# Deeper weight prefetch, 128-row bias matmuls and fewer GpSimd steps in a two-block transformer kernel

## The chip, the cores and the metric

The kernel runs on one core of a Trainium2 chip. The metric is the time of one execution on the device in microseconds. A core has five engines, each of which runs its own list of instructions in order: PE (matrix products), DVE (vectors), ACT (activations and scaled copies), POOL (GpSimd) and SP, which here only issues transfers. They wait for each other through semaphores. The DMA engines move data between HBM and the core's memory. A tile pool gives out a fixed number of buffers; a transfer into a buffer waits until its last reader is done.

## The reference

Two blocks follow each other on 512 tokens of width 1024. The first one mixes tokens with a two-directional RWKV-7 recurrence (8 heads of 64, over 256 context and 512 latent tokens) and a Fourier mix, then runs a mixture of 32 experts, top 4. The second one has two layers with three attention branches.

The recurrence, per step:

```python
sa = jnp.einsum('bhij,bhj->bhi', s, aa_t)        # aa = -kk
s = s * w_t[..., None, :] + sa[..., :, None] * bb_t[..., None, :] + v_t[..., :, None] * k_t[..., None, :]
y_t = jnp.einsum('bhij,bhj->bhi', s, r_t)
```

with `w = exp(-exp(-softplus(-w_log) - 0.5))`, whose logarithm is a constant times a sigmoid, and `a = sigmoid(...)`. An expert computes, for its tokens:

```python
u = xb @ w1[e] + b1[e]                           # 1024 -> 2048
glu = jnp.minimum(u[:, 0::2], 7.0)
lin = jnp.clip(u[:, 1::2], -7.0, 7.0)
act = glu * jax.nn.sigmoid(1.702 * glu) * (lin + 1.0)
y = act @ w2[e] + b2[e]                          # 1024 -> 1024
```

All weights are float32.

## The kernel before

The program runs through stages that show in the profile: projections (to about 160 us), the recurrence (160 to 660), output projection and routing (to 960), the experts (to 2330), the second block (to the end).

**Recurrence.** The 768 positions are six units of 128 per direction; units 0 and 1 are the context. A unit is prepared by closures in `unit()`: `lora(i)` makes the sigmoids `sw` and `a` as 0.5·tanh+0.5 (tanh on ACT, the affine on POOL, line 624), `expo1` the running sum `cum` of `sw` inside chunks of 64 (DVE scan) and on POOL the exclusive sum `cum − sw` (line 632), `expo2` three exponentials on ACT (e1 and e2 of ±cum, e3 of the exclusive sum, line 639), `keys1` to `keys4` the decayed keys: `kd`, `bk` (lines 654, 655, DVE) and `ar`, whose two halves of 64 partitions are multiplied on DVE (first) and POOL (second): lines 662 (keys by e3) and 668 (r by e1). Then follow small Gram products on PE, an inversion by substitution on DVE (lines 723, 725) with transfers in between, and the chain over chunks that carries the state (PE with POOL `pst`, line 824, and DVE). A table of positions orders the closures of different units against each other.

**Experts.** Experts are ranked by token count at run time. Rank decides the room: 192 tokens (6 experts), 128 (9, called whole) or 64 (17). Their weights come as parts of 2 × 128 rows by 512 columns, 512 KB each, 24 per expert (16 for w1, 8 for w2), 768 in all. `sequence()` and `order(g)` write out which chunks of which two to four experts alternate. Class `Weights` gives the parts in that order: `ahead()` issues loads on SP into a pool of seven raw tiles, then splits up to three parts ahead into a high half (ACT copy to fp32r, `whi`, line 1326) and a low half (DVE difference, `wlo`, line 1330), in a pool of four pairs. Parts of whole experts are used raw by PE (line 1705). `ahead()` is called at each `next()`, so in the program a load stands at most seven parts before its use; the scheduler then places each engine's instructions by priority.

For a chunk of w1, `up()` opens the PSUM tile with the bias, as a matmul: the stationary side is the expert's column of a permutation matrix, repeated (`permr`, or `mhalf` with zeros in its second half of columns for 64-token blocks, whose high and low products lie in two halves of PSUM), the moving side is `mb`, all experts' biases with 32 rows of high halves and 32 of low ones, so 64 rows (line 1837). The products follow (lines 1709, 1710, 1712). `swiglu()` then runs gl (DVE, 1727), ln (DVE, 1728), sg (ACT, 1729), ln (DVE, 1730), ln (POOL, 1731), and two PE transposes of ln (line 1690), whose copy is the input of w2. The second block has its own `Weights` with three raw tiles.

Of the kernel before, what the change touches and what calls it, by code (L numbers as in the profile page):

```python
# [8 lines left out]
F = mybir.dt.float32  # L9
# [89 lines left out]
class Blk1:  # L99
# [494 lines left out]
    def unit(self, u):  # L594
# [11 lines left out]
        def lora(i):  # L606
            def f():
                w, src, nm = ((self.w2[0], self.lw, "sw"), (self.w2[1], self.la, "a"))[i]
                dst = S[nm] = self.tt(nm)
                for d in range(2):  # L610
# [9 lines left out]
                    for hp in range(4):  # L620

                        nc.scalar.activation(dst[:, hp, 2 * d:2 * d + 2, :].rearrange("p n t -> p (n t)"), p[:, hp * 128:(hp + 1) * 128], AF.Tanh,
                                             bias=self.hb[:, i * 8 + d * 4 + hp:i * 8 + d * 4 + hp + 1], scale=0.5)
                nc.gpsimd.tensor_scalar(dst, dst, 0.5, 0.5, op0=OP.mult, op1=OP.add)
            return f

        def expo1():
            sw = S["sw"]
            c = S["c"] = self.tt("cum")
            for hp in range(4):  # L630
                nc.vector.tensor_tensor_scan(c[:, hp].rearrange("p n t -> p (n t)"), self.rst, sw[:, hp].rearrange("p n t -> p (n t)"), 0.0, OP.mult, OP.add)
            nc.gpsimd.tensor_tensor(sw, c, sw, op=OP.subtract)

        def expo2():
            sw, c = S["sw"], S["c"]
# [21 lines left out]
        def keys3():  # L657
            ar = S["ar"] = self.ubuf(u, [128, 4, 2, 4, 2, 64], "ar")
            kn = S["kn"]
            for h, e in ((0, nc.vector), (1, nc.gpsimd)):  # L660
                p = slice(h * 64, h * 64 + 64)
                e.tensor_tensor(ar[p, :, h, :, 0, :], kn[p], S["e3"][p], op=OP.mult)

        def keys4():
            ar, r = S["ar"], S["r"]
            for h, e in ((0, nc.vector), (1, nc.gpsimd)):
                p = slice(h * 64, h * 64 + 64)
                e.tensor_tensor(ar[p, :, h, :, 1, :], r[p], S["e1"][p], op=OP.mult)
            nc.gpsimd.tensor_tensor(S["kd"], S["kd"], r, op=OP.mult)
            nc.sync.dma_start(self.prD[:, u - 2].rearrange("p h d t -> p (h d t)"), S["kd"].rearrange("p h n t -> p (h n t)"))  # L670
# [625 lines left out]
class Weights:  # L1296
# [41 lines left out]

    reach = 4

    def ahead(self, loads, splits):
        while len(self.loads) < min(self.used + loads, len(self.parts)):
            m, k0 = self.parts[len(self.loads)][:2]
            self.loads.append(self.load(m(), k0))
        isplit = lambda j: self.parts[j][-1] is not False
        n = sum(isplit(j) for j in range(self.used, len(self.splits)))
        while len(self.splits) < min(len(self.loads), self.used + self.reach):
            j = len(self.splits)
            if isplit(j):
                if n >= splits:  # L1350
                    break
                n += 1
            self.splits.append(self.split(self.loads[j]) if isplit(j) else self.loads[j][0])

    def next(self, splits=None):
        self.ahead(self.nraw, self.nsplit if splits is None else splits)
        out = self.splits[self.used]
        self.used += 1
        return out


def consts_moe():
# [10 lines left out]
    lim = np.array([[float(max(128 * j, CAP[r])) if 128 * (j + 1) > CAP[r] else 1e6 for r in range(32) for j in range(4)]], np.float32)  # L1373
    two = np.concatenate([iota[:, :64], iota[:, :64]], 1)
    return {"m_cap": caps, "m_tri": tri, "m_tie": tie, "m_first": first, "m_iota": iota, "m_two": two, "m_tok": tok, "m_lim": lim}


class Moe:
# [13 lines left out]
    def consts(self):  # L1392
# [8 lines left out]
        nc.sync.dma_start(self.iota, rowbc(I["m_iota"], 512))  # L1401
        self.two = c.tile([128, 128], F, name="mtwo")
        nc.sync.dma_start(self.two, rowbc(I["m_two"], 128))
        self.tokf = c.tile([128, 5], F, name="mtokf")
# [9 lines left out]
        nc.sync.dma_start(self.br, rowbc(I["b_router"][0:1, :], 32))  # L1414
        self.cap = c.tile([128, 32], F, name="mcap")
        nc.sync.dma_start(self.cap, rowbc(I["m_cap"], 32))
        self.wr = c.tile([128, 8, 32], F, name="mwr")
        nc.sync.dma_start(self.wr, I["w_router"][0].rearrange("(k p) e -> p k e", p=128))

    def consts2(self, pool):  # L1420

        nc, I, c = self.nc, self.i, self.c
        self.halves = [c.tile([64, 128], R, name=f"mhalf{a}") for a in range(2)]
        self.b1 = c.tile([64, 2048], R, name="mb1")
        zero = pool.tile([64, 128], F, name="mz", tag="mz", bufs=1)
        nc.gpsimd.memset(zero, 0.0)
        for t in self.halves:
            nc.gpsimd.tensor_copy(t, zero)
        for a in range(2):
            t = pool.tile([128, 1024], F, name="mb1r", tag="fxh", bufs=2)  # L1430
            s = slice(a * 1024, (a + 1) * 1024)
            t = t[0:32]
            nc.sync.dma_start(t, I["b1"][0][:, s])
            nc.scalar.activation(self.b1[0:32, s], t, AF.Copy)
            nc.gpsimd.tensor_tensor(self.b1[32:64, s], t, self.b1[0:32, s].bitcast(F), op=OP.subtract)

# [55 lines left out]
    def route(self):  # L1492
# [37 lines left out]
        nc.vector.tensor_scalar(perm, self.iota[:32, :E], rank, None, op0=OP.is_equal)  # L1530
        self.perm = c.tile([64, E], R, name="permr")
        nc.vector.tensor_copy(self.perm[0:32], perm)
        nc.vector.tensor_copy(self.perm[32:64], perm)
        dr = tt.tile([32, E], F, name="drank")
# [100 lines left out]
    def hots(self, r0, n, start, two, posm=None):  # L1635

        nc = self.nc
        iob = (self.two if two else self.iota)[:, None, :128].to_broadcast([128, n, 128])
        hot = []
        for t in range(4):  # L1640
            h = self.g.tile([128, 4, 128], BF, name="hot", tag="hot", bufs=4)
            src = (self.posm if posm is None else posm)[:, t, r0:r0 + n]
            if start:
                s2 = self.g.tile([128, 8], F, name="hots", tag="hots", bufs=4)
                nc.vector.tensor_scalar(s2[:, :n], src, -float(start), None, op0=OP.add)
                src = s2[:, :n]
            nc.vector.tensor_tensor(h[:, :n], iob, src[:, :, None].to_broadcast([128, n, 128]), op=OP.is_equal)
            hot.append(h)
# [65 lines left out]
    def swiglu(self, ps, act, c, tag=None):  # L1714
# [44 lines left out]
    def plan(self, before):  # L1759
# [23 lines left out]

        first = [(lambda m=m: [m], k0) for m, k0 in before]
        self.W.stream(first + sum([parts(r, a, cc) for g in sequence() for a, r, cc in order(g)], []))

    def experts(self, hD, x1, gt2):
# [38 lines left out]
        def up(r, cc):  # L1826
# [129 lines left out]
        self.overflow(hD)  # L1956
        gs = groups()
        where = {r: min(sum(not whole(q) for q in g[:j]), 1) for g in seq for j, r in enumerate(g)}
# [52 lines left out]
    def overflow(self, hD):  # L2011
# [9 lines left out]
        with tc.If(ne > 0):  # L2021
# [19 lines left out]
            with tc.For_i(0, 128, 1) as i:  # L2041
                te = x_.tile([1, 2], I32, name="te", tag="te", bufs=1)
                nc.sync.dma_start(te, tD[bass.ds(i, 1), :])
                on = nc.values_load(te[0:1, 0:1], min_val=0, max_val=1)
                with tc.If(on > 0):
                    e = nc.values_load(te[0:1, 1:2], engines=[ET.SP], min_val=0, max_val=31)
                    ix = x_.tile([128, 1], I32, name="ix", tag="ix", bufs=1)
                    nc.sync.dma_start(ix, iD[bass.ds(i, 1), :].rearrange("a p -> p a"))
# [25 lines left out]
            nc.vector.tensor_tensor(row, self.later[3], offs[:, None, :].to_broadcast([128, 4, 32]), op=OP.add)  # L2074

            over = c.tile([128, 4, 32], F, name="over")
            nc.vector.tensor_tensor(over, self.later[3], self.cap[:, None, :].to_broadcast([128, 4, 32]), op=OP.is_ge)
            gto = self.pick(over, "gto", x_, "y")
# [1034 lines left out]
```

## Time and profile before

| | |
|---|---|
| median of 3 runs | 3734.91 us (3721.79 to 3737.12) |
| profiled execution | 3737.26 us |
| its span, first to last instruction | 3735.5 us |
| mean granted TensorE clock | 0.930 |
| PE busy | 3393.0 us (91%) |
| DVE busy | 2464.9 us (66%) |
| ACT busy | 1698.0 us (45%) |
| POOL busy | 1034.5 us (28%) |
| splits on DVE, line 1330 | 736 instructions, 883.9 us |
| splits on ACT, line 1326 | 736 instructions, 769.9 us |
| POOL's SwiGLU step, line 1731 | 152 instructions, 179.9 us |
| loads of expert weights | 768 of 512 KB |

The busy share is an average over stages with different limits, so the views below are by stage. A granted clock of 1 is 2.4 GHz, half of it 1.2 GHz. In a timeline the distance between two starts on PE says what a matmul costs; its shown length overlaps the next one. "Idle before" names what the engine waited for; where two things were waited for it is the later one.

### The profile page before, as it was taken

How to read it: one execution, taken by the hardware profiler on the slowest of the kernel's cores; microseconds unless marked ns; L12 is line 12 of the kernel's file. 1: busy time of each engine (PE TensorE's matmuls, PEld its weight loads, DVE VectorE, ACT ScalarE, POOL GpSimd, SP SyncE). 2: the span in 40 equal slices, each digit the busy share in tenths (PEclk: the TensorE clock that was granted, in tenths of full speed). 3: DMA queues.
4: the chain of work that ended last, by engine and by line, in shares of the span. 5: the costliest groups of instructions: out<-in, count | busy, mean ns of one | idle time of the engine just before them, and what ended most of it. 6: DMA issues, size and time to landing. Idle time of an engine off the chain costs nothing. (4 is left out here: it accounts for less than half of the span.)

```text
span 3735.5 us, 50031 instructions
## 1 busy us (share of the span) xinstructions
PE 3393.0 (91%) x16864; PEld 2514.0 (67%) x16864; DVE 2464.9 (66%) x4793; ACT 1698.0 (45%) x2937; POOL 1034.5 (28%) x957
## 2 busy tenths in 40 slices
PE   7966689859799999999899999799999999999999
PEld 4746576645575566656566655588878878887887
DVE  6778865676786687766687766854566455456653
ACT  4634323224555565555566554444444334344442
POOL 4444232432111112020121202432332332324223
PEclk9986667969899999999999999899999999999999
DMA  7853234626878898878989787432221243222113
GB/s 254 269 148 83 61 75 123 210 103 222 268 230 292 285 310 298 256 268 273 306 268 334 245 301 268 142 87 74 85 71 51 68 152 86 77 77 80 40 52 107
DMA packets 420639, 653.79 MB, mean 175 GB/s; under 512 B 83939, under 2 KB 145568, under 8 KB 419862
## 3 DMA queue, kind: packets, MB, share of 16 engines
q1 hardware_dynamic: 414650, 633.32, 52.6%
q0 software_dynamic: 4000, 13.90, 1.2%
q10 hardware_dynamic: 1724, 3.28, 0.3%
q8 instruction: 136, 2.23, 0.2%
q14 instruction: 129, 1.06, 0.1%
HBM read 610.80 MB, written 39.61 MB: 174 GB/s over the span
## 5 line engine op out<-in xcount | busy, mean ns | idle before, releaser
L1330 DVE TENSOR_TENSOR wlo<-wraw,whi 128x1024 fp32r<-128x1024 f32 (+1 forms) x736 | 883.9, 1210 | 417.6 <-ACT whi L1326 404.3
L1326 ACT ACTIVATE whi<-wraw 128x1024 fp32r<-128x1024 f32 x736 | 769.9, 1057 | 616.2 <-DMA wraw<-in_w 153.2
L2279 PE MATMUL psg<-whi,xh 128*128 128x512 f32 (+1 forms) x1152 | 473.1, 411 | 0.0
L2281 PE MATMUL psg<-whi,xl 128*128 128x512 f32 (+1 forms) x1152 | 451.8, 392 | 0.0
L2280 PE MATMUL psg<-wlo,xh 128*128 128x512 f32 (+1 forms) x1152 | 450.3, 391 | 0.0
L1731 POOL TENSOR_TENSOR ln<-ln,sg 64x256 f32<-64x256 f32 (+1 forms) x152 | 179.9, 1184 | 884.1 <-DVE ln L1730 464.3
L1332 POOL TENSOR_TENSOR wlo<-wraw,whi 128x288 fp32r<-128x288 f32 x184 | 241.4, 1313 | 591.8 <-ACT whi L1326 549.9
L1709 PE MATMUL ps<-whi,x 128*128 128x512 f32 x928 | 389.2, 420 | 0.7 <-ACT whi L1326 0.7
L1710 PE MATMUL ps<-wlo,x 128*128 128x512 f32 x928 | 373.9, 403 | 8.3 <-DVE wlo L1330 8.0
L1705 PE MATMUL ps<-wraw,x 128*128 128x512 f32 x576 | 270.7, 621 | 0.0
L2281 PEld LDWEIGHTS psg<-whi,xl 128*128 128x128 f32 x1152 | 217.9, 189 | 42.3
L2279 PEld LDWEIGHTS psg<-whi,xh 128*128 128x128 f32 x1152 | 218.6, 190 | 34.9 <-ACT xh L2296 0.9
L2280 PEld LDWEIGHTS psg<-wlo,xh 128*128 128x128 f32 x1152 | 218.7, 190 | 34.6
L1709 PEld LDWEIGHTS ps<-whi,x 128*128 128x128 f32 x928 | 177.7, 191 | 72.1 <-issue 22.7
L1710 PEld LDWEIGHTS ps<-wlo,x 128*128 128x128 f32 x928 | 177.9, 192 | 50.1 <-DVE wlo L1330 15.2
L1710 PE MATMUL ps<-wlo,a 128*128 128x512 f32 x464 | 193.2, 417 | 6.6 <-DVE wlo L1330 6.6
L1705 PEld LDWEIGHTS ps<-wraw,x 128*128 128x128 f32 x576 | 109.3, 197 | 131.1 <-issue 130.2
L1709 PE MATMUL ps<-whi,a 128*128 128x512 f32 x464 | 193.9, 420 | 1.0 <-ACT whi L1326 1.0
L2419 ACT ACTIVATE pexp<-pss,mx 128x128 f32<-128x128 f32 x192 | 101.1, 527 | 154.7 <-DVE mx L2414 66.7
L1705 PE MATMUL ps<-wraw,a 128*128 128x512 f32 x288 | 136.5, 611 | 0.0
L1677 POOL DMA_INDIRECT xg<-hD,idxi x38 | 40.4, 1062 | 288.7 <-PE ps L1690 271.2
L1710 PEld LDWEIGHTS ps<-wlo,a 128*128 128x128 f32 x464 | 90.6, 195 | 36.9 <-DVE wlo L1330 14.9
(736 smaller groups left out, 6850.2 us busy)
## 6 DMA issues: line engine op xcount, KB each, us to landing
wraw<-in_w SPq DMA_DIRECT2D x768, 512.0 KB
wraw<-in_w_in SPq DMA_DIRECT2D x140, 512.0 KB
mraw<-in_w_ada SPq DMA_DIRECT2D x32, 512.0 KB
wraw<-in_w_out SPq DMA_DIRECT2D x24, 512.0 KB
wada<-in_w_ada SPq DMA_DIRECT2D x16, 512.0 KB
wraw<-in_w_mem_kv SPq DMA_DIRECT2D x16, 512.0 KB
wraw<-in_w_branch_m SPq DMA_DIRECT2D x8, 512.0 KB
wraw<-in_w_branch_b SPq DMA_DIRECT2D x8, 512.0 KB
```

The lines of the kernel that those rows point to most:

```text
L1326: nc.scalar.activation(hi, raw, AF.Copy)
L1330: nc.vector.tensor_tensor(lw[:, :m], rw[:, :m], hw[:, :m].bitcast(F), op=OP.subtract)
L1332: nc.gpsimd.tensor_tensor(lw[:, m:], rw[:, m:], hw[:, m:].bitcast(F), op=OP.subtract)
L1677: self.last = nc.gpsimd.indirect_dma_start(out=x[:n], out_offset=None, in_=hD, in_offset=bass.IndirectOffsetOnAxis(ap=idx, axis=0))
L1705: nc.tensor.matmul(ps, a, w[:, k], start=s, stop=e)
L1709: nc.tensor.matmul(ps, a, hi[:, k], start=s, stop=False)
L1710: nc.tensor.matmul(ps, a, lo[:, k], start=False, stop=e and not two)
L1731: nc.gpsimd.tensor_tensor(ln[:m], ln[:m], sg[:m], op=OP.mult)
L2279: nc.tensor.matmul(p, xh[:, kk], hi[:, k, :n], start=kk == 0, stop=False)
L2280: nc.tensor.matmul(p, xh[:, kk], lo[:, k, :n], start=False, stop=False)
L2281: nc.tensor.matmul(p, xl[:, kk], hi[:, k, :n], start=False, stop=kk == kch - 1)
L2419: nc.scalar.activation(p[:, :n], s[:, :n], AF.Exp, bias=nm, scale=-1.0, accum_out=H["d"][:, i:i + 1])
```

## The change

Four edits. Weight loads: eight raw tiles instead of seven, and `ahead()` issues loads, before and after the splits, until the tile that the next one reuses has not yet been split (or, for raw parts, used). Until the expert loop begins a limit holds the loads to seven parts past the first ones. First biases: `mb` holds columns 0 to 1023 in rows 0 to 63 and columns 1024 to 2047 in rows 64 to 127, and the permutation column is zero in the other 64 rows, so the matmul contracts over 128 rows; `mhalf` becomes two tiles per set, hence two POOL copies per expert that uses it. Memory for this comes from a broadcast iota and from sharing one tag for gl and sg. Recurrence: the affine goes to ACT, the exclusive sum and its exponential are dropped (the exclusive decay is e1 shifted by one position, with the first column copied), and both halves of keys3 and keys4 run on DVE.

```diff
@@ unit(), lora / expo1 / expo2 / keys3 / keys4
-                nc.gpsimd.tensor_scalar(dst, dst, 0.5, 0.5, op0=OP.mult, op1=OP.add)
+                nc.scalar.activation(dst, dst, AF.Copy, bias=0.5, scale=0.5)
...
-            nc.gpsimd.tensor_tensor(sw, c, sw, op=OP.subtract)
...
-            nc.scalar.activation(sw, sw, AF.Exp, scale=-KAP)
-            S["e3"] = sw
...
-            for h, e in ((0, nc.vector), (1, nc.gpsimd)):
+            for h in range(2):
                 p = slice(h * 64, h * 64 + 64)
-                e.tensor_tensor(ar[p, :, h, :, 0, :], kn[p], S["e3"][p], op=OP.mult)
+                nc.vector.tensor_tensor(ar[p, :, h, :, 0, 1:], kn[p, :, :, 1:], S["e1"][p, :, :, :63], op=OP.mult)
+                nc.gpsimd.tensor_copy(ar[p, :, h, :, 0, 0], kn[p, :, :, 0])
...
-            for h, e in ((0, nc.vector), (1, nc.gpsimd)):
+            for h in range(2):
                 p = slice(h * 64, h * 64 + 64)
-                e.tensor_tensor(ar[p, :, h, :, 1, :], r[p], S["e1"][p], op=OP.mult)
+                nc.vector.tensor_tensor(ar[p, :, h, :, 1, :], r[p], S["e1"][p], op=OP.mult)
@@ class Weights
-    def __init__(self, tc, ctx, raw=7, parts=4, kn=2, side="left"):
+    def __init__(self, tc, ctx, raw=8, parts=4, kn=2, side="left"):
...
     def ahead(self, loads, splits):
-        while len(self.loads) < min(self.used + loads, len(self.parts)):
-            m, k0 = self.parts[len(self.loads)][:2]
-            self.loads.append(self.load(m(), k0))
         isplit = lambda j: self.parts[j][-1] is not False
+        def fetch():
+            top = min(len(self.parts), self.limit or len(self.parts))
+            while len(self.loads) < top:
+                j = len(self.loads)
+                q = j - self.nraw
+                if j >= self.used + loads if loads else q >= 0 and q >= (len(self.splits) if isplit(q) else self.used):
+                    break
+                m, k0 = self.parts[j][:2]
+                self.loads.append(self.load(m(), k0))
+        fetch()
...
+        fetch()
     def next(self, splits=None):
-        self.ahead(self.nraw, self.nsplit if splits is None else splits)
+        self.ahead(0 if self.free else self.nraw, self.nsplit if splits is None else splits)
@@ Moe.consts2, Moe.swiglu, Moe.plan, up()
-        self.b1 = c.tile([64, 2048], R, name="mb1")
+        self.b1 = c.tile([128, 1024], R, name="mb1")
...
-        gl = x_.tile([128, 256], F, name="gl", tag="gl", bufs=2)
+        gl = x_.tile([128, 256], F, name="gl", tag="gl", bufs=3)
...
-        sg = x_.tile([128, 256], F, name="sg", tag="sgm", bufs=2)
+        sg = x_.tile([128, 256], F, name="sg", tag="gl", bufs=3)
...
+        self.W.free, self.W.limit = False, len(first) + 7
...
-                nc.gpsimd.tensor_copy(half[:, 0:64], self.perm[:, r:r + 1].bitcast(F).to_broadcast([64, 64]))
+                for a in range(2):
+                    nc.gpsimd.tensor_copy(half[a][:, 0:64], self.perm[:, a, r:r + 1].bitcast(F).to_broadcast([128, 64]))
...
-                        pm = half if xx.n == 64 else self.perm[:, r:r + 1].to_broadcast([64, 128])
-                        nc.tensor.matmul(p, pm, self.b1[:, cc * 512:(cc + 1) * 512], start=True, stop=False)
+                        pm = half[cc // 2] if xx.n == 64 else self.perm[:, cc // 2, r:r + 1].to_broadcast([128, 128])
+                        nc.tensor.matmul(p, pm, self.b1[:, cc % 2 * 512:(cc % 2 + 1) * 512], start=True, stop=False)
```

The change also moves instructions. On ACT, in the experts, this is the place whose `sg` for a 64-token block starts at 1317.18 us in the trace of before (whi: high half of a part; sg: sigmoid of SwiGLU; us: first half of a 64-token sum; a: transposed activations). Before:

```order
L1693 ACTIVATE a<-ps 128x2x64
L1326 ACTIVATE whi<-wraw 128x1024 x4
L1729 ACTIVATE sg<-gl 128x256
L1326 ACTIVATE whi<-wraw 128x1024 x3
L1720 ACTIVATE us<-ps 64x512
L1326 ACTIVATE whi<-wraw 128x1024 x2
L1693 ACTIVATE a<-ps 128x256
L1729 ACTIVATE sg<-gl 64x256
L1326 ACTIVATE whi<-wraw 128x1024
L1720 ACTIVATE us<-ps 64x512
```

After, where line 1738 is sg, 1729 is us and 1325 is whi:

```order
L1702 ACTIVATE a<-ps 128x2x64
L1325 ACTIVATE whi<-wraw 128x1024 x2
L1738 ACTIVATE sg<-gl 128x256
L1325 ACTIVATE whi<-wraw 128x1024 x4
L1729 ACTIVATE us<-ps 64x512
L1325 ACTIVATE whi<-wraw 128x1024 x3
L1702 ACTIVATE a<-ps 128x256
L1729 ACTIVATE us<-ps 64x512
L1325 ACTIVATE whi<-wraw 128x1024
L1738 ACTIVATE sg<-gl 64x256
```

Counted from the start of the experts, three more high halves now stand ahead of this sg, and so does the next block's us.

On POOL, in the recurrence, the preparation of the second latent unit between two steps of the chain (pst). Before:

```order
L624 TENSOR_SCALAR sw<-sw 128x1024
L624 TENSOR_SCALAR a<-a 128x1024
L632 TENSOR_TENSOR sw<-cum,sw 128x1024
L642 COPY pcc<-e_2760 128x16
L824 TENSOR_TENSOR pst<-sv,pcc 64x256 x2
L668 TENSOR_TENSOR ar<-r,e_2760 64x4x4x64
L662 TENSOR_TENSOR ar<-kn,sw 64x4x4x64
L824 TENSOR_TENSOR pst<-sv,pcc 64x256 x2
L649 TENSOR_TENSOR a<-a,kn 128x1024
L650 TENSOR_TENSOR kd<-kd,k 128x1024
```

After:

```order
L661 COPY ar<-kn 64x4x4 x2
L639 COPY pcc<-e_2757 128x16
L823 TENSOR_TENSOR pst<-sv,pcc 64x256 x4
L646 TENSOR_TENSOR a<-a,kn 128x1024
L647 TENSOR_TENSOR kd<-kd,k 128x1024
```

Five long operations leave POOL; the two products of keys3 and keys4 stand on DVE instead.

## Rows read from the trace of the kernel before

**Rows 1.** Table by stage: PE, PEld, DVE, ACT, POOL busy us (instructions), clock, DMA share, GB/s.

```profile
160.00:660.00 500.00, 375.91 (x3241) 306.10 (x3240) 363.74 (x774) 174.83 (x388) 193.84 (x179) 0.71 0.41 108
...
960.00:2330.00 1370.00, 1295.97 (x4767) 832.36 (x4768) 998.49 (x1444) 759.08 (x1046) 218.00 (x190) 0.97 0.83 280
```

**Rows 2.** Same view, a 50-us window of the experts.

```profile
1950.00:2000.00 50.00, 50.00 (x175) 30.52 (x174) 33.44 (x51) 27.44 (x39) 9.40 (x9) 1.00 0.97 338
```

**Rows 3.** Waits, 960 to 2330 us: engine, line, waited for: us, times, longest.

```profile
ACT whi L1326 <- DMA wraw<-in_w: 148.1, 133, 7.2
...
PE ps L1690 <- POOL ln L1731: 41.3, 15, 5.2
...
PE ps L1710 <- DVE wlo L1330: 14.5, 20, 3.1
```

**Rows 4.** Timeline, PE at 1676 us: start, length, instruction, count, [idle before <-releaser].

```profile
1676.43 0.44 PE L1690 MATMUL ps<-ident,ln 128*128 128x128 f32 x2 [3.75 <-POOL ln L1731]
...
1678.20 0.63 PE L1709 MATMUL ps<-whi,x 128*128 128x512 f32 x1
1678.63 0.63 PE L1710 MATMUL ps<-wlo,x 128*128 128x512 f32 x1
```

**Rows 5.** Same view, PE at 2101 to 2107 us.

```profile
2101.20 0.34 PE L1690 MATMUL ps<-ident,ln 64*128 64x64 f32 x2
2101.47 0.50 PE L1709 MATMUL ps<-whi,x 128*128 128x512 f32 x1
...
2104.46 0.33 PE L1690 MATMUL ps<-ident,ln 64*128 64x64 f32 x2
2104.61 0.48 PE L1837 MATMUL ps<-mb,permr 64*128 64x512 f32 x1
2105.01 0.50 PE L1709 MATMUL ps<-whi,x 128*128 128x512 f32 x1
...
2106.05 0.39 PE L1710 MATMUL ps<-wlo,x 128*128 128x512 f32 x1
2106.28 0.39 PE L1712 MATMUL ps<-whi,x 128*128 128x512 f32 x1
2106.60 0.50 PE L1837 MATMUL ps<-mb,mhalf 64*128 64x512 f32 x1
2107.03 0.50 PE L1709 MATMUL ps<-whi,x 128*128 128x512 f32 x1
```

**Rows 6.** Instructions of line 1837: count, shortest/median/longest ns, first and last start.

```profile
L1837 PEld LDWEIGHTS ps<-mb,mhalf x92: 182/183/336, 826.1 to 2284.2; 64*128 64x128 f32 x92
...
L1837 PE MATMUL ps<-mb,permr x60: 469/478/793, 822.5 to 2296.4; 64*128 64x512 f32 x60
```

**Rows 7.** Timeline, ACT at 1317 us.

```profile
1317.18 0.40 ACT L1729 ACTIVATE sg<-gl 64x256 f32<-64x256 f32 x1
...
1320.97 1.05 ACT L1326 ACTIVATE whi<-wraw 128x1024 fp32r<-128x1024 f32 x1
```

**Rows 8.** Groups by line, POOL, 160 to 660 us: count, busy us, mean ns, idle before.

```profile
L662 POOL TENSOR_TENSOR ar<-kn,sw 64x1024 f32<-64x1024 f32 x6 | 16.1, 2689 | 13.6 <-PE ps L867 12.1 <-issue 1.4
...
L632 POOL TENSOR_TENSOR sw<-cum,sw 128x1024 f32<-128x1024 f32 x6 | 14.7, 2456 | 18.3 <-DVE cum L631 11.5 <-DVE Fm L725 6.8
...
L668 POOL TENSOR_TENSOR ar<-r,e 64x1024 f32<-64x1024 f32 x4 | 10.7, 2666 | 0.2
...
L624 POOL TENSOR_SCALAR a<-a 128x1024 f32<-128x1024 f32 x6 | 6.6, 1101 | 3.3 <-ACT a L622 3.3
```

**Rows 9.** Same view, DVE, 160 to 660 us.

```profile
L654 DVE TENSOR_TENSOR bk<-a,e 128x1024 f32<-128x1024 f32 x6 | 13.7, 2279 | 10.3 <-POOL a L649 10.2
...
L668 DVE TENSOR_TENSOR ar<-r,e 64x1024 f32<-64x1024 f32 x4 | 13.0, 3249 | 0.0
...
L662 DVE TENSOR_TENSOR ar<-kn,sw 64x1024 f32<-64x1024 f32 x6 | 9.9, 1655 | 0.1
...
L655 DVE TENSOR_TENSOR bk<-kd,e 128x1024 f32<-128x1024 f32 x6 | 7.3, 1212 | 0.0
```

More of the change, by code (lines that the diff above doesn't have):

```diff
@@ L1337, in stream @@
         self.parts, self.loads, self.splits, self.used = parts, [], [], 0
-    reach = 4
+    reach, free = 4, True
+    limit = None
     def ahead(self, loads, splits):
-        while len(self.loads) < min(self.used + loads, len(self.parts)):
-            m, k0 = self.parts[len(self.loads)][:2]
-            self.loads.append(self.load(m(), k0))
         isplit = lambda j: self.parts[j][-1] is not False
+        def fetch():
[8 more added lines that the diff above has]
+        fetch()
         n = sum(isplit(j) for j in range(self.used, len(self.splits)))
@@ L1373, in consts_moe @@
     lim = np.array([[float(max(128 * j, CAP[r])) if 128 * (j + 1) > CAP[r] else 1e6 for r in range(32) for j in range(4)]], np.float32)
-    two = np.concatenate([iota[:, :64], iota[:, :64]], 1)
-    return {"m_cap": caps, "m_tri": tri, "m_tie": tie, "m_first": first, "m_iota": iota, "m_two": two, "m_tok": tok, "m_lim": lim}
+    return {"m_cap": caps, "m_tri": tri, "m_tie": tie, "m_first": first, "m_iota": iota, "m_tok": tok, "m_lim": lim}
 class Moe:
@@ L1401, in consts @@
         nc.sync.dma_start(self.iota, rowbc(I["m_iota"], 512))
-        self.two = c.tile([128, 128], F, name="mtwo")
-        nc.sync.dma_start(self.two, rowbc(I["m_two"], 128))
         self.tokf = c.tile([128, 5], F, name="mtokf")
@@ L1414, in consts @@
         nc.sync.dma_start(self.br, rowbc(I["b_router"][0:1, :], 32))
-        self.cap = c.tile([128, 32], F, name="mcap")
-        nc.sync.dma_start(self.cap, rowbc(I["m_cap"], 32))
         self.wr = c.tile([128, 8, 32], F, name="mwr")
@@ L1422, in consts2 @@
         nc, I, c = self.nc, self.i, self.c
-        self.halves = [c.tile([64, 128], R, name=f"mhalf{a}") for a in range(2)]
-        self.b1 = c.tile([64, 2048], R, name="mb1")
-        zero = pool.tile([64, 128], F, name="mz", tag="mz", bufs=1)
+        self.halves = [[c.tile([128, 128], R, name=f"mhalf{a}{b}") for b in range(2)] for a in range(2)]
+        self.b1 = c.tile([128, 1024], R, name="mb1")
+        zero = pool.tile([128, 1024], F, name="mb1r", tag="fxh", bufs=2)[:, :128]
         nc.gpsimd.memset(zero, 0.0)
-        for t in self.halves:
+        self.perm = c.tile([128, 2, 32], R, name="permr")
+        nc.gpsimd.tensor_copy(self.perm.rearrange("p c e -> p (c e)"), zero[:, :64])
+        for t in self.halves[0] + self.halves[1]:
             nc.gpsimd.tensor_copy(t, zero)
@@ L1431, in consts2 @@
             s = slice(a * 1024, (a + 1) * 1024)
[L1432 to L1435, printed above, removed]
+            p = slice(a * 64, a * 64 + 32)
+            nc.sync.dma_start(t[p], I["b1"][0][:, s])
+            nc.scalar.activation(self.b1[p], t[p], AF.Copy)
+            nc.gpsimd.tensor_tensor(self.b1[a * 64 + 32:a * 64 + 64], t[p], self.b1[p].bitcast(F), op=OP.subtract)
     def logits(self, t, hT):
@@ L1530, in route @@
         nc.vector.tensor_scalar(perm, self.iota[:32, :E], rank, None, op0=OP.is_equal)
-        self.perm = c.tile([64, E], R, name="permr")
-        nc.vector.tensor_copy(self.perm[0:32], perm)
-        nc.vector.tensor_copy(self.perm[32:64], perm)
+        for a in range(4):
+            nc.vector.tensor_copy(self.perm[a * 32:a * 32 + 32, a // 2], perm)
         dr = tt.tile([32, E], F, name="drank")
@@ L1637, in hots @@
         nc = self.nc
-        iob = (self.two if two else self.iota)[:, None, :128].to_broadcast([128, n, 128])
+        a = 2 if two else 1
+        iob = self.iota[:, None, None, :128 // a].to_broadcast([128, n, a, 128 // a])
         hot = []
@@ L1956, in experts @@
         self.overflow(hD)
+        self.W.limit, self.W.free = None, True
         gs = groups()
@@ L2041, in overflow @@
             with tc.For_i(0, 128, 1) as i:
-                te = x_.tile([1, 2], I32, name="te", tag="te", bufs=1)
+                te = x_.tile([1, 2], I32, name="te", tag="ix", bufs=1)
                 nc.sync.dma_start(te, tD[bass.ds(i, 1), :])
@@ L2046, in overflow @@
                     e = nc.values_load(te[0:1, 1:2], engines=[ET.SP], min_val=0, max_val=31)
-                    ix = x_.tile([128, 1], I32, name="ix", tag="ix", bufs=1)
+                    ix = x_.tile([128, 1], I32, name="ix", tag="te", bufs=1)
                     nc.sync.dma_start(ix, iD[bass.ds(i, 1), :].rearrange("a p -> p a"))
@@ L2074, in overflow @@
             nc.vector.tensor_tensor(row, self.later[3], offs[:, None, :].to_broadcast([128, 4, 32]), op=OP.add)
+            cap = x_.tile([128, 32], F, name="mcap", tag="te", bufs=1)
+            nc.sync.dma_start(cap, rowbc(I["m_cap"], 32))
             over = c.tile([128, 4, 32], F, name="over")
-            nc.vector.tensor_tensor(over, self.later[3], self.cap[:, None, :].to_broadcast([128, 4, 32]), op=OP.is_ge)
+            nc.vector.tensor_tensor(over, self.later[3], cap[:, None, :].to_broadcast([128, 4, 32]), op=OP.is_ge)
             gto = self.pick(over, "gto", x_, "y")
```

4 lines of the change are left out of this document (2 added, 2 removed).

## The prediction

> **What bounds the kernel now.** I read the table by stage first [rows 1]. In the recurrence (160 to 660 us) PE is busy 376 of 500 us at a mean granted clock of 0.71 and DVE 364: the two take turns. In the experts (960 to 2330) PE is busy 1296 of 1370 us, the DMA engines 0.83 of the time at 280 GB/s. So an edit pays there where it shortens PE's own work or one of its waits. Then 50-us windows of the experts: at 1950:2000 DMA is full (share 0.97, 338 GB/s) and PE is busy all 50 us [rows 2], so either may end last there. Next, the waits of that stage [rows 3]: PE waits 41.3 us (15 times) for POOL's last step of the SwiGLU (ln) and 14.5 us (20 times) for DVE's low halves; ACT waits 148.1 us (133 times, 1.1 us each) for weights to land, most of which never reaches PE. Last, PE in order of time [rows 4]: behind a wait of 3.75 us matmuls start 0.43 us apart, 0.23 when the clock is full [rows 5].
>
> The profiled execution took 3737.3 us, 2.4 us over the median of the runs shown; the sum is made against it and carried to that median by −2.
>
> **First biases over 128 rows.** Rows 5 price this directly. Where a matmul of 128 rows precedes the bias: it starts 2106.28, the bias 2106.60, the next 2107.03: 0.75 us for two steps that cost 0.23 each between 128-row matmuls (2106.05 to 2106.28). With 128 rows 0.46 is left: 0.29 saved. Where a pair of 64-row transposes precedes it: 2104.46, 2104.61, 2105.01, 0.55 in all. There the switch of rows only moves ahead of the bias: at 2101.20 the 128-row matmul behind such a pair starts 0.27 later, and with 0.23 behind it 0.50 is left: 0.05 saved. There are 92 biases of 64-token blocks and 60 of others [rows 6]. By PE's order of time 62 follow a 128-row matmul, 41 a 128-row transpose (counted like the former) and 49 a 64-row one: 103 × 0.29 + 49 × 0.05 = 32 us. PE's order around them is unchanged.
>
> Not all of that reaches the end. Of the biases 29 start in 50-us windows whose DMA share is 0.9 or more; where PE runs ahead there, it waits for a load instead. I keep four fifths: −25. The ends are −32 and −15 (the gain only of the 73 in windows with a share under 0.8). The second POOL copy of 23 experts lies beside PE's matmuls of the expert before. It has 64 elements per row; if that cover is gone and it took as long as DVE's pass of 1024 [rows 9], it would cost 23 × 1.21 = 28 us, since PE waits for POOL's ln behind it. I take 0: at 64 elements it is a small part of that.
>
> The Trainium skill, page "TensorE: Matmul & The Clock Gate", section "LDWEIGHTS (loading the stationary operand)", says that a 32-row weight load takes as long as a 128-row one: only its columns count. The trace agrees for the load alone (183 ns, rows 6). By that rule this edit gains nothing, and the sum would be 25 us smaller. But the rows show the cost in the starts on either side of a change of rows, and those decide.
>
> **The eighth raw tile and earlier loads.** Earlier places in SP's order change little by themselves, since SP's loads already wait for a tile to come free. What counts is one tile more: 512 KB at 338 GB/s take 1.55 us, so a late load comes at most that much earlier, against a mean wait of ACT of 1.1 us. Gain at PE: half of the 14.5 us, 7. The chain gl, sg, ln runs on DVE, ACT and POOL between splits, and a split that is done earlier is out of its way: about 0.4 us of each of the 15 waits, 6. Behind a wait some 9 matmuls cost 0.2 us more; two waits avoided or halved give 3. Together −16.
>
> Against that stands the order. The scheduler now places 1 to 4 more splits ahead of 44 of the SwiGLU steps on ACT. In the trace 12 of these have no slack: PE's transposes start within 0.6 us of POOL's ln. One is shown: sg starts at 1317.18, the third split behind it at 1320.97 [rows 7], and three more splits now go first. A split whose load is there costs ACT 1.05 us (rows 7); the 19 at those 12 steps make 20 us, and I count half, because some will be done before the step is ready: +10. Net −6. The ends: −30 (all of the 14.5 and a third of the 41.3 us), and +60, the rival (c).
>
> **Recurrence units.** POOL loses 12 affines (1.1 us), 6 subtracts (2.46) and the second halves of keys3 and keys4 (16.1 and 10.7 us) [rows 8]: 55 of its 194 us. ACT gets 12 passes of 1.05 us and loses 6: +6 on 175 busy us, beside PE and DVE. DVE gets both halves: 20 passes; where POOL is silent one of 1024 elements takes 1.21 us (L655, rows 9), so 24 us, against 9.9 + 13.0 now for ten, because L668 ran at 3.25 us beside POOL's half. L654, of the same shape as L655, takes 2.28 [rows 9]: 6 us that come back in part. So DVE has about as much to do as before. Each unit's preparation loses one POOL step of 2.46 us and the wait for POOL's slow half. That reaches the end only where preparation is late, and PE's clock of 0.71 says that the stretch is a chain of short turns rather than work. I take −8, 1.3 us per unit. The ends are −25 (half of POOL's 55 us lay on the path) and +15 (ten new halves of 1.21 us land on the path, and a little more for ACT).
>
> The page "SBUF — State Buffer", section "Who interferes with whom", calls this contention an exclusive lock between a DVE instruction with two SBUF inputs and a GpSimd one that reads SBUF. The trace agrees in sign (2.28 against 1.21 us); with all of POOL's 55 us as blocked DVE time, the end of −25 would be −55, and no row carries that.
>
> **What stays.** The second block keeps three raw tiles, and its first wait, behind ACT's layer norm, has the same order. The broadcast iota, the shared buffers of gl and sg, and the perm copies lie off PE's path: 0.
>
> **Sum.** −25 − 6 − 8 = −39: 3737.3 − 39 − 2 = 3696 us.
>
> **Rivals.** (a) Everything pays: the biases 32, the tile 30, the recurrence 20, so 3655. For it: where DMA has room, PE's own work is the bound, and 32 of the 82 us are its work. Against it: the 41.3 us are mostly the latency of the SwiGLU chain, not late loads.
>
> (b) The gain is swallowed: DMA is the bound often enough, or the switch of rows costs as much ahead of the bias as behind it, or the loads ran as far ahead as they will. Then −5 to −18, about 3725. For it: 0.97 in rows 2, and SP's present waits. Against it: 280 GB/s in the stage leave 17% of 338.
>
> (c) Slower: the moved splits. If loads land no earlier than now, sg waits for them: at the 12 steps without slack 1.1 to 7.2 us each, 38 us by ACT's present starts, and 12 × 1.8 us of matmuls at the lower clock: +60. Less 33 for biases and recurrence that is +27, so 3762. It decides from about 3 us per step on. For it: share 0.97 in places. Against it: the tile is worth 1.55 us per load, and the other 32 steps have 3.7 to 14 us of slack.
>
> **How the numbers follow.** About 0.5% (19 us) is what a measurement can tell from no change: under 3716 is faster, over 3754 slower. Forecast, with its own range of 3670 to 3716: 0.54; (a) 0.14; (b) 0.22; (c) 0.10. A little of (b) lies under 3716, a little of (c) under 3754: faster 0.71, same 0.20, slower 0.09. The range reaches through most of (a) and (b): 3650 to 3738.
>
> **What would show it.** Right: bias matmuls whose successor starts 0.23 us later; fewer than 20 PE waits for low halves; DVE's new halves at about 1.21 us and L654's successor near it. Wrong: PE's waits for ln over 55 us with an ACT split directly ahead of sg, which is (c); a DMA share as before while PE's waits for splits rise, which is (b); and a recurrence as long as before, which puts its −8 at 0.

## The result and the profile after

The changed kernel takes 3676.61 us (median of 4 runs, 3674.06 to 3677.72) against 3735.08 us before on the same chip: ratio 0.985, 95% interval 0.9826 to 0.9873. That is 58 us less; 3696 us were predicted, with a range of 3650 to 3738. The profiled execution has a span of 3675.4 us, 60.1 less.

Four marks in the two profiles say in which stage the time went. All are in us from the start of the span; the differences are worked out from them.

| | before | after | difference in the stage |
|---|---|---|---|
| last state update of the recurrence (POOL pst ends) | 600.7 | 587.5 | −13.2 |
| first expert bias on PE | 822.5 | 815.1 | +5.8, so −7.4 so far |
| last matmul of the experts' combine ends | 2333.1 | 2278.6 | −47.1 |
| end | 3735.5 | 3675.4 | −5.6 |

By stage, after (columns as in [rows 1]); the experts end 54 us earlier, so their window is 960 to 2276. The last two lines are the whole experts' stage, from the first bias to the last combine matmul, before and after:

```profile
160.00:660.00 500.00, 378.15 (x3314) 307.19 (x3312) 364.31 (x809) 182.79 (x400) 152.20 (x165) 0.73 0.41 109
960.00:2276.00 1316.00, 1251.66 (x4753) 837.42 (x4752) 987.78 (x1425) 754.63 (x1042) 214.31 (x206) 0.97 0.86 291
...
822.00:2333.00 1511.00, 1423.67 (x5284) 913.56 (x5284) 1099.65 (x1647) 824.42 (x1141) 251.09 (x216) 0.97 0.82 275
...
815.00:2279.00 1464.00, 1373.32 (x5284) 919.93 (x5284) 1094.72 (x1647) 822.51 (x1142) 247.74 (x238) 0.96 0.84 284
```

Over the whole stage PE is busy 50 us less (1373 instead of 1424) and idle about as long as before (91 instead of 87 us). So the gain there is shorter work on PE and not, on balance, shorter waits. From 960 us on DMA brings 291 instead of 280 GB/s and its share rises from 0.83 to 0.86. POOL in the recurrence falls from 194 to 152 us, DVE stays at 364.

PE in order of time. First the second product behind each place of [rows 5], in the trace of before:

```profile
2101.80 0.40 PE L1710 MATMUL ps<-wlo,x 128*128 128x512 f32 x1
...
2105.35 0.40 PE L1710 MATMUL ps<-wlo,x 128*128 128x512 f32 x1
...
2107.37 0.40 PE L1710 MATMUL ps<-wlo,x 128*128 128x512 f32 x1
```

Then the places after that answer to [rows 5] (line 1848 is the bias, 1699 a transpose, 1718, 1719 and 1721 the products):

```profile
2050.81 0.33 PE L1699 MATMUL ps<-ident,ln 64*128 64x64 f32 x2
2051.08 0.50 PE L1718 MATMUL ps<-whi,x 128*128 128x512 f32 x1
2051.42 0.40 PE L1719 MATMUL ps<-wlo,x 128*128 128x512 f32 x1
...
2054.08 0.33 PE L1699 MATMUL ps<-ident,ln 64*128 64x64 f32 x2
2054.34 0.49 PE L1848 MATMUL ps<-mb,permr 128*128 128x512 f32 x1
2054.67 0.39 PE L1718 MATMUL ps<-whi,x 128*128 128x512 f32 x1
2054.90 0.40 PE L1719 MATMUL ps<-wlo,x 128*128 128x512 f32 x1
...
2055.84 0.40 PE L1721 MATMUL ps<-whi,x 128*128 128x512 f32 x1
2056.07 0.40 PE L1848 MATMUL ps<-mb,mhalf 128*128 128x512 f32 x1
2056.30 0.40 PE L1718 MATMUL ps<-whi,x 128*128 128x512 f32 x1
2056.54 0.40 PE L1719 MATMUL ps<-wlo,x 128*128 128x512 f32 x1
```

Behind a 128-row matmul the bias now starts 0.23 us later and its successor 0.23 after it, as [rows 5] let expect. Behind 64-row transposes it is 0.26 and 0.33, in all 0.59 us where it was 0.55. But the second matmul behind a bias counts too. Before, it started 0.34 us after the first one (2107.03 to 2107.37, 2105.01 to 2105.35); now it is 0.23 or 0.24 (2056.30 to 2056.54, 2054.67 to 2054.90). From the matmul ahead of the bias to the second one behind it, the first place falls from 1.09 to 0.70 us, and the place behind the transposes from 0.89 to 0.82. The product that follows such a pair of transposes without a bias had its successor 0.33 us later before (2101.47 to 2101.80) and has it 0.34 later now (2051.08 to 2051.42).

The instructions of the bias line ([rows 6]) have the same counts, and a weight load takes 188 ns instead of 183.

```profile
L1848 PEld LDWEIGHTS ps<-mb,mhalf x92: 186/188/338, 819.1 to 2231.8; 128*128 128x128 f32 x92
```

Waits of the experts' stage ([rows 3]), with the two lines of the whole stage (822 to 2333 us before, 815 to 2279 after) at the end:

```profile
ACT whi L1325 <- DMA wraw<-in_w: 110.4, 91, 6.0
...
PE ps L1699 <- POOL ln L1740: 39.9, 15, 5.2
...
PE ps L1719 <- DVE wlo L1329: 9.8, 9, 3.1
...
PE ps L1690 <- POOL ln L1731: 53.1, 19, 5.2
...
PE ps L1699 <- POOL ln L1740: 61.9, 22, 5.2
```

ACT waits 38 us less for weights, and PE waits for low halves 9 times instead of 20. PE's waits for POOL's ln stay from 960 us on: 39.9 us, 15 times. Over the whole stage they rise from 53.1 to 61.9 us.

This is the place of [rows 7], ACT in order of time. The high halves that were placed ahead of sg run before gl is there, and sg waits for DVE's gl:

```profile
1294.02 2.95 ACT L1325 ACTIVATE whi<-wraw 128x1024 fp32r<-128x1024 f32 x3
...
1297.89 1.05 ACT L1325 ACTIVATE whi<-wraw 128x1024 fp32r<-128x1024 f32 x1
1299.58 0.42 ACT L1738 ACTIVATE sg<-gl 64x256 f32<-64x256 f32 x1 [0.65 <-DVE gl L1736]
```

PE at the same place waits 0.25 us for ln:

```profile
1302.15 0.33 PE L1699 MATMUL ps<-ident,ln 64*128 64x64 f32 x2 [0.25 <-POOL ln L1740]
```

POOL's groups in the recurrence ([rows 8]; line 668 is kd times r, 661 the first column), count, busy us, mean ns, idle before:

```profile
L668 POOL TENSOR_TENSOR kd<-kd,r 128x1024 f32<-128x1024 f32 x4 | 13.3, 3316 | 29.1 <-DVE bk L652 24.6 <-issue 4.4
...
L661 POOL COPY ar<-kn 64x16 f32<-64x16 f32 x12 | 6.1, 506 | 12.9 <-DMA kn<-knD 7.4 <-PE ps L866 5.0
```

DVE's groups there ([rows 9]):

```profile
L660 DVE TENSOR_TENSOR ar<-kn,e 64x1008 f32<-64x1008 f32 x12 | 19.9, 1654 | 0.7 <-ACT e L636 0.6
...
L667 DVE TENSOR_TENSOR ar<-r,e 64x1024 f32<-64x1024 f32 x8 | 11.8, 1476 | 0.2
L651 DVE TENSOR_TENSOR bk<-a,e 128x1024 f32<-128x1024 f32 x6 | 11.6, 1933 | 2.2 <-POOL a L646 2.2
...
L652 DVE TENSOR_TENSOR bk<-kd,e 128x1024 f32<-128x1024 f32 x6 | 7.3, 1211 | 0.0
```

DVE's new halves take 1.65 and 1.48 us on average, not 1.21; L651 (L654 of before) takes 1.93 instead of 2.28. These four lines together take 50.6 us, 43.9 before. The means hide two kinds. Of the twenty new halves sixteen took 1.19 to 1.22 us. Four took 2.5 to 3.3 us: these began while a POOL product was running, and each ended 1.05 to 1.08 us after that product did. DVE and POOL in order of time show both:

```profile
293.21 5.78 DVE L660 TENSOR_TENSOR ar<-kn,e 64x1008 f32<-64x1008 f32 x2
...
302.54 1.22 DVE L667 TENSOR_TENSOR ar<-r,e 64x1024 f32<-64x1024 f32 x1
...
294.62 3.31 POOL L647 TENSOR_TENSOR kd<-kd,k 128x1024 f32<-128x1024 f32 x1
302.58 3.37 POOL L668 TENSOR_TENSOR kd<-kd,r 128x1024 f32<-128x1024 f32 x1 [4.66 <-DVE bk L652]
```

The two halves at 293.21 run beside POOL's products and take 5.78 us together. The half at 302.54 begins 0.04 us before POOL's product and takes 1.22.

### The profile page after: what moved, and what is told of

Read it like the earlier page. It is cut to its first block, busy times and chain, and to the rows that moved or that the text cites. A ratio compares the mean times of both kernels' runs of the same rounds, so it can differ in the third digit from the quotient of the medians.

```text
span 3675.4 us, 50079 instructions
## 1 busy us (share of the span) xinstructions
PE 3329.5 (91%) x16864; PEld 2509.5 (68%) x16864; DVE 2453.5 (67%) x4805; ACT 1699.2 (46%) x2943; POOL 983.8 (27%) x967
## 5 line engine op out<-in xcount | busy, mean ns | idle before, releaser
L1718 PE MATMUL ps<-whi,x 128*128 128x512 f32 x928 | 377.6, 407 | 0.2 <-ACT whi L1325 0.2
L1740 POOL TENSOR_TENSOR ln<-ln,sg 64x256 f32<-64x256 f32 (+1 forms) x152 | 158.8, 1045 | 811.7 <-DVE ln L1739 523.4
L1738 ACT ACTIVATE sg<-gl 64x256 f32<-64x256 f32 (+1 forms) x152 | 62.8, 413 | 117.4 <-DVE gl L1736 112.6
L1923 PE MATMUL ps<-y,ot 128*128 128x512 f32 x424 | 116.2, 411 | 0.0
```

The lines of the kernel that those rows point to most:

```text
L1718: nc.tensor.matmul(ps, a, hi[:, k], start=s, stop=False)
L1740: nc.gpsimd.tensor_tensor(ln[:m], ln[:m], sg[:m], op=OP.mult)
L1923: nc.tensor.matmul(p, ot[j][:, t * 128:(t + 1) * 128], part, start=j == 0 and i == 0, stop=j == n - 1 and i == len(y) - 1)
```

## The experiments

Each experiment was timed in five rounds beside the kernel before, whose median was 3727.8 us beside the first four, 3730.9 beside the next four and 3733.6 beside the last three. So medians compare within such a group, and ratios across groups. In the first group the kernel with "loads placed as before" can stand for the changed kernel. The stage column is from each kernel's one profile: first bias to the last combine matmul (1510.6 before). With the late bias a product comes first, 5.6 and 7.9 us ahead of the first bias, and the column counts from there.

| | ratio to before (95%) | median us | experts' stage us |
|---|---|---|---|
| changed kernel | 0.985 (0.9826 to 0.9873) | 3676.6 | 1463.5 |
| 64-row biases again | 0.9949 (0.993 to 0.9967) | 3707.1 | 1496.8 |
| old units again | 0.989 (0.9872 to 0.9908) | 3685.8 | 1464.7 |
| seven raw tiles again | 0.9913 (0.9896 to 0.993) | 3696.6 | 1480.3 |
| loads placed as before, eight tiles | 0.9869 (0.9851 to 0.9887) | 3677.5 | 1460.7 |
| biases alone | 0.9951 (0.9936 to 0.9965) | 3713.4 | 1486.2 |
| units alone | 0.9994 (0.9981 to 1.0007) | 3728.6 | 1506.3 |
| eighth tile and loads alone | 0.9955 (0.994 to 0.997) | 3714.9 | 1497.5 |
| bias behind the first products | 0.9839 (0.9823 to 0.9854) | 3670.5 | 1456.8 |
| second halves of keys on POOL | 0.9884 (0.9864 to 0.9905) | 3689.6 | 1470.6 |
| last SwiGLU step on DVE | 0.983 (0.9813 to 0.9848) | 3668.0 | 1456.3 |
| that and the late bias | 0.9803 (0.9786 to 0.9819) | 3657.7 | 1454.4 |

**64-row biases again.** The bias contracts over the 64 rows of the new storage that hold the values:

```diff
+                        hs = slice(cc // 2 * 64, cc // 2 * 64 + 64)
-                        pm = half[cc // 2] if xx.n == 64 else self.perm[:, cc // 2, r:r + 1].to_broadcast([128, 128])
+                        pm = half[cc // 2][hs] if xx.n == 64 else self.perm[hs, cc // 2, r:r + 1].to_broadcast([64, 128])
```

(The moving side is `self.b1[hs, ...]`.)

> The changed kernel, except that the first biases contract over 64 rows again (the half of the new storage that holds the values). Theory: the bias edit is worth its PE time, 24.4 us less in the trace, nearly all of which reaches the end: 3697 to 3703. Rival (DMA swallows a good part of what PE gains): 3685 to 3692. Rival (the edit is worth nothing at the end, the gain in the experts is all prefetch): 3676 to 3680.

Measured 3707.1, above the theory's range: a loss of 37 us by the ratios (0.9949 against 0.985), 30 by the medians (also against "loads placed as before" from the same rounds), 33 in the experts' stage. Both rivals fall. The 24.4 us of the expectation are too little. They count starts on PE from the matmul ahead of each bias to the one behind it (99.6 us before, 75.2 in the changed kernel). To the second one behind it the 152 biases take 162.3 us before and 121.8 after: the edit is worth some 40 us of PE's time.

This kernel's biases are not quite the old ones. The values of columns 1024 to 2047 now lie in the upper 64 rows, and 30 of the 49 biases behind 64-row transposes now start 0.006 us after the first transpose and ahead of the second; none does in the kernel before:

```profile
2077.97 0.27 PE L1699 MATMUL ps<-ident,ln 64*128 64x64 f32 x1
2077.97 0.50 PE L1849 MATMUL ps<-mb,permr 64*128 64x512 f32 x1
2078.08 0.22 PE L1699 MATMUL ps<-ident,ln 64*128 64x64 f32 x1
```

From the last product ahead of bias and transposes to the second product behind, without PE's waits, the biases' places take 206 us before, 202 here and 165 in the changed kernel. So 37 us of PE's time are given up here, and 30 to 37 reach the end.

**Old units again.** The lines of the diff for `unit()` taken back.

> The changed kernel with the recurrence units of before. Theory: the last state update came 13 us earlier and the first bias 7 us earlier, so undoing it costs 7 to 13 us: 3684 to 3690. Rival (the routing stage ends at the same time whatever the units do): 3674 to 3680. Rival (the units also change what the experts start from): above 3692.

Measured 3685.8, in the theory's range: 8 us more than "loads placed as before" in the same rounds, 9 more than the changed kernel by the medians, 0.4% or 15 us by the ratios. The last state update comes at 595.0 us instead of 587.5.

**Seven raw tiles again.** `raw=8` to `raw=7`.

> The changed kernel with seven raw tiles instead of eight, loads still issued as far ahead as tiles allow. Theory (the tile is what counts, earlier places in the program are not): the experts lose the 20 us of shorter stalls: 3692 to 3700. Rival (the earlier places of loads and splits in the order made the gain): 3676 to 3682. My forecast's own share for the tile was 6 us: 3683.

Measured 3696.6, 19 us more than with eight tiles in the same rounds, and the experts' stage is 17 us longer. That is the theory, and three times my own share. The waits of that kernel, 960 to 2276 us, show where:

```profile
ACT whi L1325 <- DMA wraw<-in_w: 162.1, 134, 7.0
...
PE ps L1699 <- POOL ln L1740: 36.2, 13, 5.1
...
PE ps L1719 <- DVE wlo L1329: 20.1, 29, 3.1
```

Against the changed kernel PE waits 20.1 instead of 9.8 us for low halves (29 times instead of 9) and ACT 162 instead of 110 for weights. The waits for ln are 4 us shorter with seven tiles. Over the whole stage PE is idle 100 us instead of 91 and busy 1380 instead of 1373. With seven tiles the scheduler also puts the splits back: ahead of 150 of the 152 sg steps stand as many as before the change, and in the next kernel, with eight tiles and the old loads, they stand as in the changed one. So the tile, not the earlier loads, moved them.

**Loads placed as before.**

```diff
-    reach, free = 4, True
+    reach, free = 4, False
...
-        self.W.limit, self.W.free = None, True
+        self.W.limit, self.W.free = None, False
```

> The changed kernel with eight raw tiles, but loads placed in the program at most eight parts before their use, as before, and not as far ahead as splits allow. Theory (SP waits for tiles anyway, so the place is nothing): 3673 to 3681. Rival (the place decides, since the scheduler moved splits with it): 3690 to 3700, as if the tile were not there.

Measured 3677.5, with 1460.7 us in the experts: the place is nothing there, as predicted. But the second block, which uses the same class with three tiles, took 1400.1 us from the last combine matmul to the end. In the profiles of the four kernels with the old placing it is 1400.1 to 1402.8, in those of the nine with the new one 1394.6 to 1397.6. There the placing is worth some 5 us.

**One part alone.** The biases alone, the units alone, and the tile with the loads alone (biases over 64 rows of the new storage):

> The kernel before with only the biases over 128 rows (and the memory rearranged for them); seven raw tiles, loads and units as before. Theory: PE is the bound of the experts even with seven tiles, so the bias edit alone is worth what undoing it cost, 25 to 33 us: ratio to before 0.991 to 0.9935. Rival (without the eighth tile PE runs into late loads): 8 to 15 us, ratio 0.996 to 0.998.

> The kernel before with only the new recurrence units. Theory: 7 to 13 us by the earlier end of the chain, experts and second block as before: ratio 0.9965 to 0.998. Rival (the gain of the units needs the other edits): 0.999 to 1.001.

> The kernel before with only the eighth raw tile and the earlier loads; biases over 64 rows (in the new storage), units as before. Theory: the tile alone takes 17 to 22 us from the experts: ratio 0.994 to 0.9955. Rival (splits moved ahead of SwiGLU steps eat it when PE is slower at the biases): 0.998 to 1.002.

Biases alone: 0.49%, 18 us (13 to 24), between theory and rival. In its profile the experts' stage is 24.4 us shorter. PE is busy 35 us less there (1388.7 against 1423.7) and idle 10 us more (97 against 87), and its waits for low halves rise from 14.5 us, 20 times, to these:

```profile
PE ps L1708 <- DVE wlo L1330: 20.7, 31, 3.1
```

So with seven tiles a part of what the biases save goes into waits. The tile alone: 0.45%, 17 us, at the edge of the theory; 13.1 us in the stage and 5.6 in the second block. Up to 3 us of the 13.1 are biases that start beside transposes, as in the 64-row kernel. The units alone: no gain that the interval tells from none, so the theory missed, although that profile's recurrence ends 15 us earlier; its 12 runs spread from 3720 to 3741. Alone the parts make 1.0% together, in company 1.5%. The waits that the biases run into with seven tiles, and the eighth takes away, are one reason; how much of the difference they make was not settled.

**Bias behind the first products.**

```diff
-                    if k0 == 0:
+                    self.mm_part(p, xx, w, k0, k0 == 0, k0 + kn == 8)
+                    if k0 == kn:
...
-                        nc.tensor.matmul(p, pm, ..., start=True, stop=False)
+                        nc.tensor.matmul(p, pm, ..., start=False, stop=False)
-                    self.mm_part(p, xx, w, k0, False, k0 + kn == 8)
```

> The changed kernel with each first bias added behind the chunk's first two products instead of ahead of them; the sum is the same. In the changed kernel a bias behind transposes has its successor 0.32 to 0.34 us later, elsewhere 0.23. Theory (the weight load behind two short transposes is not covered by them, whatever comes next): the 0.1 us moves to the product that now follows the transposes, time 3672 to 3680, bias successors 0.23 us everywhere. Rival (it belongs to the bias): 90 times 0.1 us less, 3664 to 3669.

```profile
2042.73 0.40 PE L1721 MATMUL ps<-whi,x 128*128 128x512 f32 x1
2042.96 0.39 PE L1849 MATMUL ps<-mb,permr 128*128 128x512 f32 x1
2043.19 0.40 PE L1718 MATMUL ps<-whi,x 128*128 128x512 f32 x1
...
2053.75 0.33 PE L1699 MATMUL ps<-ident,ln 64*128 64x64 f32 x2
2054.01 0.49 PE L1718 MATMUL ps<-whi,x 128*128 128x512 f32 x1
2054.35 0.39 PE L1719 MATMUL ps<-wlo,x 128*128 128x512 f32 x1
```

Line 1849 is the bias. It costs 0.23 us now (2042.73, 2042.96, 2043.19), and the product behind the transposes has its successor 0.34 later (2054.01 to 2054.35), as the bias had. On PE that is the theory. The time, 3670.5, lies between theory and rival, with an interval that overlaps the changed kernel's, and decides for neither.

**Second halves of keys on POOL.** `for h, e in ((0, nc.vector), (1, nc.gpsimd))` again in keys3 and keys4, the rest of the units new.

> The changed kernel, but the second halves of keys3 and keys4 on POOL again (the shifted decay and the affine on ACT stay). In the profiles the new units end the recurrence some 8 us earlier. Theory (the gain is DVE freed from POOL's halves and POOL's slow halves off the path): the last state update comes 4 to 8 us later, 3680 to 3686. Rival (the gain is the subtract and the third exponential that are gone): 3674 to 3679, the last update within 2 us.

Measured 3689.6, above the theory's 3680 to 3686, with the last state update at 594.3, 6.8 us later and as late as with the old units (595.0). So the direction is the theory's, the loss about 13 us. The dropped subtract and exponential show no gain, as far as one profile each and intervals of some 15 us can tell. DVE's own time does not explain the loss: it is lower here, 351.5 us busy in 160 to 660 against 364.3.

**The last SwiGLU step on DVE, and both together.** `nc.gpsimd.tensor_tensor(ln[:m], ln[:m], sg[:m], ...)` becomes `nc.vector.tensor_tensor`.

> The changed kernel with the last step of SwiGLU, ln times sg, on DVE instead of POOL. PE still waits 61.9 us (22 times) for that step. Theory (these waits are the latency of the SwiGLU chain, in which POOL's 0.7 to 1.6 us is the slowest link): PE's waits for ln fall to 35 to 50 us and the time to 3655 to 3668. Rival (DVE's queue is the link: the step then stands behind low halves): waits as before or longer, 3674 to 3690.

> The last step of SwiGLU on DVE and the first bias behind the chunk's first products together. If both help on their own they add: 3650 to 3664. If the late bias is only noise: as the kernel with the DVE step alone, within 4 us.

With the step on DVE alone, 3668.0, at the edge of the theory. The interval overlaps the changed kernel's, so the time alone does not tell the two apart. PE's waits for the step, over the whole stage (813 to 2269 us):

```profile
PE ps L1699 <- DVE ln L1740: 41.3, 16, 5.2
```

DVE's group of that line in the same kernel, whole span:

```profile
L1740 DVE TENSOR_TENSOR ln<-ln,sg 64x256 f32<-64x256 f32 (+1 forms) x152 | 63.3, 417 | 16.6 <-ACT sg L1738 11.1 <-DVE ln L1739 0.5
```

The step takes 0.42 us instead of 1.05 on POOL. PE's waits fall from 61.9 to 41.3 us over the stage, inside the theory's 35 to 50. The rival, longer waits, falls. Here the scheduler also moved splits ahead of 63 sg steps instead of 44, so the edit is not the step alone. Both together give 3657.7, ratio 0.9803 (0.9786 to 0.9819): faster than the changed kernel, just beyond both intervals, and the fastest version here. Against the DVE step alone, in the same rounds, the late bias added 10 us, and the runs do not overlap (3655 to 3660 against 3664 to 3672). In the profiles only 2 of them lie in the experts' stage (1456.3 to 1454.4); what the late bias gains by was not settled.

## Why the prediction was right, and where its terms were off

The direction and the places were right: experts first, recurrence second. The sum was 39 and the change brought 58 to 60. Taken back one at a time in the same rounds, the parts are worth 30 us (biases), 19 (tile) and 8 (units) where 25, 6 and 8 were predicted.

**Biases, −25 predicted.** Two steps were off, in opposite directions. First, the price stopped one matmul too early. The second matmul behind a 64-row bias also started late, 0.34 us after the first instead of 0.23. Counted to there, by medians, a bias behind a 128-row matmul (62 of 152) or a 128-row transpose (41) saved 0.39 us, not 0.29. Behind a 64-row pair (49) it saved 0.05, as predicted, but not as reasoned: "with 0.23 behind it 0.50 is left" misses the row behind 2101.47, which starts 0.33 us later. The edit's PE time is some 40 us, not 32. Second, "I keep four fifths" was too much for the biases alone: 18 us by the time and 24 in the stage, while PE's idle time grew by 10. With the eighth tile it was about right: 30 to 37 us reach the end. So −25 is near partly by luck. The second POOL copy was put at 0 because it is "a small part" of 1.21 us. The copies of that line took 0.29 us in the median (46, up to 3.95), and PE's weight loads wait for them 0.7 us in all, so the 0 held. The end of −15 counts 73 biases in windows with a DMA share under 0.8; by those windows they are about 65, which moves that end by 2 us.

The Trainium skill, page "TensorE: Matmul & The Clock Gate", section "LDWEIGHTS (loading the stationary operand)", says that only the columns of a weight load count. That held for the load (188 against 183 ns); that the edit would therefore gain nothing is excluded by the biases alone, 0.9951.

**Eighth tile, −6 predicted.** The mechanism was right, its size was three times as large: 17 us in the stage and 19 in time by taking it back, 13 in the stage alone. Two terms were mis-sized. The gain at low halves, "half of the 14.5 us", was put at 7; against seven tiles in the same kernel, whose shorter biases had brought these waits to 20.9 us over the stage, they fall to 9.8, those for high halves from 3.8 to 0.2, and PE is busy 7 us less. And the 6 us by which the waits for ln should shrink did not come: they are 61.9 us against 56.4 with seven tiles. The +10 for splits ahead of SwiGLU steps was near. At the 44 steps with more splits ahead, PE's idle time before the transposes is 35.9 us, against 26.6 before and 30.3 with seven tiles; at the other 108 it stays at 26. At the place of [rows 7] itself the splits cost little, since they had run before gl was ready.

**Units, −8 predicted.** The recurrence ends 13.2 us earlier in these two profiles, but single profiles scatter. The six with all of the new units and the bias in its old place have the first bias at 808.5 to 815.1 us, the four with the old units at 818.9 to 822.5: 9 us earlier by the means (the two with the late bias begin with a product at 819.3 and 807.4). Taking the units back cost 8 to 15 us, the units alone gained 2 (none by their interval). The size fits these, which is not a sharp test. "DVE has about as much to do" held (364 us busy both times), and so did 1.21 us for sixteen of the twenty new halves. The other four ran into a POOL product. POOL lost 42 us, not 55, since twelve small copies take 6 and kd times r went from 2.80 to 3.32 us each. The kernel with the slow halves on POOL again points to their leaving the path as what pays.

**What stays, 0 predicted.** The wait at the start of the second block did stay:

```profile
PE psg L2293 <- ACT memh L2514: 15.8, 1, 15.8
```

But the second block gained 5 us by the placing of its loads, which I had called nothing.

**Rivals.** (a) came about as near as the forecast, 22 us below the result where the forecast was 19 above (its own sum, 82 us off, gives 3653). (b) is out with its 18 us at most; a part of it shows in the biases alone, whose PE time went partly into waits. (c) is out by the result. With seven tiles the splits stand as before and the time is longer, so the tile brings more than the moved splits cost.

## What to carry to other kernels

On an in-order PE price a small matmul by the starts around it, from the one ahead to two behind, since the cost of changing its shape sits in its neighbours and is paid again one instruction later. A prefetch buffer was worth here what the waits at its end cost together with the slow matmuls after them. It also moves instructions: splits ahead of a critical one cost little where their data were there and the engine would have idled, and some 6 to 9 us of PE's waits over 44 places. Before a step is taken from GpSimd, ask whether PE waits for it. The keys' halves paid, by the one kernel that put them back; SwiGLU's last product shortened PE's waits, with a gain in time that only the kernel with the late bias shows clearly; dropping work off the path showed no gain.

## What was not expected of the hardware

After two short transposes the second matmul starts late, 0.32 us behind the first after 128-row ones (0.34 after 64-row ones) instead of 0.23, whatever the first one is: a product before the change, a bias after it, a product again in the kernel with the late bias. The weight load of 0.19 us has then only transposes of 0.11 us each to hide behind. That this is the reason was not tried by itself, and the second matmul behind a 64-row bias starts 0.34 us after the first too, without any transpose near.

A change from 128 to 64 rows costs 0.09 us behind a product and 0.17 behind a transpose, one from 64 to 128 rows 0.12 (behind transposes) to 0.19 us (behind a bias), by the starts in the traces before and after, and 0.1 more at the matmul after that behind a bias.

In the 64-row kernel 30 biases start 0.006 us after a 64-row transpose. That these are the biases in the upper rows, which such a transpose leaves free, was not tried. And a DVE product with two inputs that began while a POOL product ran ended 1.05 to 1.08 us after it, while one that began first took its usual 1.2 us.
